# Loading the first rows of a rotation kernel in three pieces instead of two

## Chip, cores, metric

The kernel runs on one core of one Trainium2 chip. The metric is the device time of an execution in microseconds (us). A kernel is timed in rounds that alternate with the kernel before on the same chip. A profile covers one execution, and its span is some 1.8 us shorter than the time. Several figures below come from the trace's single packet records (start, duration and size of every packet) where no table of stretches shows them.

## The reference

The output is the input with both image axes reversed:

```python
x = randn(32, 3, 256, 256)                 # float32
out = rot90(x, k=2, axes=(-2, -1))         # out[.., i, j] = x[.., 255-i, 255-j]
```

The 96 images are 25.17 MB. They have to be read once and written once, so 50.33 MB pass through the DMA engines.

## The kernel before

The images are taken as three strips, A, Bt and Ct, of 32 images each. A strip is 128 rows of 16384 floats: every image is cut into four rows of 64 KB, one to each SBUF partition. VectorE reverses every row in place through a buffer T, and the store writes the four rows of an image in reverse order.

```python
G = 32
E = L // 4                                  # 16384 floats: 64 KB a row
x4 = x.rearrange("b c h w -> (b c) (h w)").rearrange(
    "(g n) (s e) -> g (n s) e", n=G, s=4)   # rows are 64 KB apart in memory
# ...
def load(t, g, lo, hi, queue=nc.sync):
    return queue.dma_start(out=t[:, lo:hi], in_=x4[g][:, lo:hi])
# ...
TAIL = 1536
HEAD = 512                                  # 2 KB of each row
load(A, 0, 0, HEAD, nc.scalar)
load(A, 0, HEAD, E)
load(Bt, 1, 0, E)
body = load(Ct, 2, 0, E - TAIL)
load(Ct, 2, E - TAIL, E)
inside(A)                                   # 12 copies on VectorE
LEAD = 128
store(A, 0, 0, LEAD)
first = store(A, 0, LEAD, E)                # made to wait for `body`
# ...
for g, t in ((1, Bt), (2, Ct)):
    inside(t)
    store(t, g, 0, E)
```

The large store of A is issued only when Ct's first load, `body`, has landed, so the loads come first and the stores after them. And VectorE's first copy of a strip reads the end of the row, which the largest load brings.

## Time and profile before

| | before |
|---|---|
| time, median of the first 3 runs | 122.09 us (121.94 to 122.15) |
| span of the profile | 120.2 us |
| sixteen DMA engines, share of the span with a packet | 97.6% |
| VectorE busy | 37% |
| VectorE's first copy starts | 22.6 us |

The DMA engines are the bound. Each has eight rows of each large load, and handles a row as one packet. The useful view is therefore the table of stretches, laid around the moments at which all sixteen engines take their next row (a "wave"). In such a stretch, DMA share times length is the mean packet time that one engine took on, and GB/s times length is the bytes, hence the number of packets. The prediction shows these lines.

### The profile page before, as it was taken

Reading aid. Unit: us, or ns where it says so; the run is one execution under the profiler, and the core shown is the slowest. Engines: PE = TensorE matmul, PEld = TensorE weight load, DVE = VectorE, ACT = ScalarE, POOL = GpSimd, SP = SyncE. Lnnn points to the kernel's source line nnn. Section 1 sums busy time; section 2 is a strip of 40 time slices with the busy share of each in tenths; the row PEclk is TensorE's granted clock in tenths of the full one; section 3 lists DMA queues with packets and bytes.
Section 4 is the critical chain, followed back from the end, with each engine's and each line's share of the span. In section 5 each row is a group of like instructions: output and inputs, shape, how many; then the busy total and the mean of one; then the engine's idle time right before and its main releaser. Section 6 shows DMA issues by size and latency. Waiting matters only on the chain.

```text
span 120.2 us, 97 instructions
## 1 busy us (share of the span) xinstructions
DVE 44.2 (37%) x36; POOL 0.2 (0%) x4
## 2 busy tenths in 40 slices
DVE  0000000499995099999059999500000000000000
POOL 0000000000000000000000000000000000000000
DMA  9888988899889879979499777988898889888990
GB/s 338 349 349 349 698 349 349 360 654 393 349 349 633 382 316 553 395 316 633 178 452 693 346 346 346 693 349 349 349 698 349 349 349 698 349 349 349 654 393 0
DMA packets 1296, 50.33 MB, mean 419 GB/s; under 512 B 144, under 2 KB 272, under 8 KB 528
## 3 DMA queue, kind: packets, MB, share of 16 engines
q1 hardware_dynamic: 1152, 50.07, 97.0%
q10 hardware_dynamic: 144, 0.26, 0.6%
HBM read 25.17 MB, written 25.17 MB: 419 GB/s over the span
## 4 chain that ended last, share of the span: by engine, by line
DMA 34%; DVE 25%; another core or an unknown queue 4%; issue 1%; SPq 0%; DVEq 0%
DMA Bt<-in_x_dram 34%; DVE T L52 8%; DVE Bt L52 8%; DVE Ct L52 8%; SPq L55 0%; DVEq L52 0%
## 5 line engine op out<-in xcount | busy, mean ns | idle before, releaser
L52 DVE COPY T<-A 128x2048 f32<-128x2048 f32 x4 | 4.9, 1226 | 22.7 <-DMA A<-in_x_dram 22.6
L52 DVE COPY T<-Ct 128x2048 f32<-128x2048 f32 x4 | 4.9, 1227 | 4.5 <-DMA Ct<-in_x_dram 4.4
L52 DVE COPY T<-Bt 128x2048 f32<-128x2048 f32 x4 | 4.9, 1226 | 4.4 <-DMA Bt<-in_x_dram 4.3
L52 DVE COPY Bt<-Bt 128x2048 f32<-128x2048 f32 x4 | 4.9, 1227 | 0.1
L52 DVE COPY A<-A 128x2048 f32<-128x2048 f32 x4 | 4.9, 1227 | 0.1
L52 DVE COPY A<-T 128x2048 f32<-128x2048 f32 x4 | 4.9, 1227 | 0.1
L52 DVE COPY Bt<-T 128x2048 f32<-128x2048 f32 x4 | 4.9, 1227 | 0.1
L52 DVE COPY Ct<-T 128x2048 f32<-128x2048 f32 x4 | 4.9, 1227 | 0.1
L52 DVE COPY Ct<-Ct 128x2048 f32<-128x2048 f32 x4 | 4.9, 1227 | 0.1
L100 POOL MEMSET const-bfloat16-1.0<- 128x1 bf16 x1 | 0.1, 101 | 0.0
L100 POOL MEMSET const-uint8-127<- 128x1 uint8 x1 | 0.1, 101 | 0.0
L100 POOL MEMSET const-float32-0.0<- 128x1 f32 x1 | 0.1, 98 | 0.2 <-issue 0.2
L100 POOL MEMSET const-float32-1.0<- 128x1 f32 x1 | 0.1, 98 | 0.0
## 6 DMA issues: line engine op xcount, KB each, us to landing
out_dram<-A SPq DMA_DIRECT2D x1, 8128.0 KB, 21.1
A<-in_x_dram SPq DMA_DIRECT2D x1, 7936.0 KB, 21.9
Ct<-in_x_dram SPq DMA_DIRECT2D x1, 7424.0 KB, 57.9
Ct<-in_x_dram SPq DMA_DIRECT2D x1, 768.0 KB, 59.3
A<-in_x_dram ACTq DMA_DIRECT2D x1, 256.0 KB, 22.0
out_dram<-A SPq DMA_DIRECT2D x1, 64.0 KB, 35.2
Bt<-in_x_dram SPq DMA_DIRECT2D x1, 40.8
out_dram<-Bt SPq DMA_DIRECT2D x1, 39.8
```

The source lines that it names most:

```text
L52: tc.keep_in_program_order(nc.vector.tensor_copy(out=dst, in_=src))
L100: nc = _bacc.Bacc("TRN2", target_bir_lowering=False, num_devices=1)
```

## The change

The intent is that the first packets are short on both queues, so that the engines get going at once, with the large rows behind them.

```diff
     load(A, 0, 0, HEAD, nc.scalar)
-    load(A, 0, HEAD, E)
+    load(A, 0, HEAD, 2 * HEAD)
+    load(A, 0, 2 * HEAD, E)
     load(Bt, 1, 0, E)
```

## The prediction

> **What bounds the kernel now.** I read the page first, for who is busy.
>
> ```profile
> span 120.2 us, 97 instructions
> DVE 44.2 (37%) x36; POOL 0.2 (0%) x4
> DMA packets 1296, 50.33 MB, mean 419 GB/s; under 512 B 144, under 2 KB 272, under 8 KB 528
> q1 hardware_dynamic: 1152, 50.07, 97.0%
> q10 hardware_dynamic: 144, 0.26, 0.6%
> ```
>
> VectorE works 37% of the span; the sixteen DMA engines are taken 97.0 + 0.6 = 97.6% of it. Every byte must come in and go out once, and the change alters none of that, so all that it can touch is the 2.4% (2.9 us over all, start and end included) in which the DMA engines hold no packet, and the way their time divides into packets. q10 is ACT's load: 144 packets are 128 rows and 16 small ones for completion, nine on each engine. q1 is SyncE's: eight transfers of 144.
>
> Next, who waits, to see whether VectorE's idle time is a reason or a result.
>
> ```profile
> DVE T L52 <- DMA A<-in_x_dram: 22.6, 1, 22.6
> DVE T L52 <- DMA Ct<-in_x_dram: 4.4, 1, 4.4
> DVE T L52 <- DMA Bt<-in_x_dram: 4.3, 1, 4.3
> ```
>
> VectorE waits once for each strip, always for a load, so it keeps up. Its last copy ends at about 76.7 us, while the stores of the first strip are still on the queue. The strips' arrival is only important in so far as the DMA engines never run dry.
>
> Then SyncE's own instructions in the timeline, for the start and for the turn from loads to stores.
>
> ```profile
> 0.73 0.39 SPq L55 DMA_DIRECT2D A<-in_x_dram  x1
> 1.18 0.42 SPq L55 DMA_DIRECT2D Bt<-in_x_dram  x1
> ...
> 26.39 33.78 SPq L58 DMA_DIRECT2D out_dram<-A  x2
> ```
>
> The first load is issued in 0.39 us, and about 0.45 us lies between two issues. (ACT issues its 2 KB piece at the same 0.73 us.) The second row says that the big store of A is out by 60.2 us. The question is whether the queue has work all the way, and the table of stretches answers it (columns: stretch, length, VectorE, GpSimd, clock, DMA share, GB/s). A stretch counts packets that begin in it, so I chose stretches around the waves in which all sixteen engines change packets.
>
> ```profile
> 1.20:1.75 0.55, 0.00 (x0) 0.00 (x0) 1.00 0.00 0
> 1.75:2.15 0.40, 0.00 (x0) 0.00 (x0) 1.00 7.23 2381
> 2.75:2.90 0.15, 0.00 (x0) 0.00 (x0) 1.00 0.98 423
> 4.70:5.35 0.65, 0.00 (x0) 0.00 (x0) 1.00 3.73 1613
> 24.10:24.75 0.65, 0.65 (x1) 0.00 (x0) 1.00 3.72 1613
> 59.25:60.25 1.00, 0.00 (x0) 0.00 (x0) 1.00 1.03 430
> 118.70:119.10 0.40, 0.00 (x0) 0.00 (x0) 1.00 0.02 0
> 119.10:120.18 1.08, 0.00 (x0) 0.00 (x0) 1.00 0.00 0
> ```
>
> - No packet begins before 1.75 us. In 1.75 to 2.15, 2381 GB/s for 0.40 us is 952 KB, which is 15 rows of 62 KB. Their time is 7.23 x 0.40 x 16 / 15 = 3.08 us each. The sixteenth engine begins in 2.75 to 2.90 and takes 0.98 x 0.15 x 16 = 2.35 us. The ACT pieces are not there: they wait until the big row is through.
> - At 4.70 to 5.35, 16 rows of 62 KB and 16 pieces of 2 KB start (1613 x 0.65 = 1048 KB = 16 x 64 KB): 3.73 x 0.65 = 2.42 us per engine for both. A 64 KB row of Bt (24.10 to 24.75) takes 3.72 x 0.65 = 2.418 us.
> - So the first wave costs about 3.08 - 2.34 = 0.74 us too much (2.34 being 62 KB at the steady pace), on fifteen engines. Afterwards the pace is steady.
> - At 59.25 to 60.25, the tail of Ct: 430 KB are 70 packets of 6 KB, 1.03 x 1.00 x 16 / 70 = 235 ns each. From 6 KB at 235 ns and 64 KB at 2418 ns, a packet costs 9 ns plus its bytes at 27.2 GB/s; sixteen engines make 435 GB/s.
> - The last completions begin by 119.10, and 1.08 us follows to the end of the span.
>
> The bound is therefore the stream of packets on each engine, from 1.76 us to 119.05: 3.146 MB per engine at 27.2 GB/s is 115.6 us, 72 data packets at 9 ns are 0.65, nine completion packets under 0.1, the start-up 0.74. That gives 117.1 of 117.3 us.
>
> **What the Trainium skill says.** "DMA: Bandwidth & Descriptors", section Bandwidth, puts the fabric's ceiling at 16 x 32 B x 850 MHz = 435.2 GB/s; the fit above gives 435, so nothing is to be had from the steady part. The same page, section Queues, rings and completion order, says that an engine takes its queues in turn, a whole packet at a time; the trace agrees, with one 2 KB piece after each 62 KB row at 4.70 to 5.35. Its section Issuing engines are not separate DMA queues says that issuing from several engines saves only the sequencer's time, since all run on the same sixteen engines. Its section Latency and other measured facts gives about 600 ns to the first byte for a transfer issued from SyncE or ACT; here the issue ends at 1.12 and the first packet begins at 1.76, 0.64 us later.
>
> **The change, part by part.**
> 1. Removed: the single load of 62 KB per row. Added: one of 2 KB and one of 60 KB in its place. Bytes are unchanged. Each engine has eight rows, so eight more packets at 9 ns, plus one completion packet of about 9 ns: 8 x 9 + 9 = 81 ns. These lie on the path, because each engine's stream sets the end: +0.08 us.
> 2. Added: one issue on SyncE, 0.45 us. All later loads are issued 0.45 us later (Bt at about 1.63 instead of 1.18). The queue holds work until then (step 4), so +0.00 on the path. The stores wait for data and for Ct's load, not for this.
> 3. Moved: the first 0.5 MB. Every engine begins with 2 KB pieces of both queues in turn. At (9 + 75) = 84 ns a piece, the sixteen pieces of an engine take 1.34 us, and only then do the 60 KB rows begin, near 3.1 us without the start-up and near 3.9 us with it. The order of the bytes changes, not their number: 0.00.
> 4. Does an engine run dry? Its first packets come 1.76 - 0.73 = 1.03 us after the issue. The 60 KB load, issued at 1.18, is there at about 2.2 us. The eight SyncE pieces alone last to 1.76 + 0.67 = 2.43 even without any start-up, with ACT's to 3.1. No gap: 0.00.
> 5. The start-up of 0.74 us is what the change could aim at. I take it for a delay of the first reads that is paid once, however long the first packet is: a first packet of 2 KB would last 0.08 + 0.7 us in place of 2.34 + 0.74. The engine that started late, near 2.8, paid nothing and still finished its row together with the others, which looks as if no data moved before about 2.5 us for anybody. I give a part of it a chance: expected gain 0.15 us.
> 6. VectorE: the last byte of A is still behind the same number of bytes, so it starts at 22.6 to 22.7 us. Its slack behind Bt (4.3 us) and Ct (4.4 us) absorbs that.
>
> Sum: +0.08 - 0.15 = -0.07, hence 122.09 - 0.07 = 122.0 us.
>
> **Rivals.**
> - The start-up belongs to large first packets (sixteen reads of 62 KB set off at once) and short ones avoid it. For it: 3.08 against 2.34 us, and that the sixteenth engine, alone in starting, took 2.35. Against: the early engines' lost time looks like one delay common to them all. The time would be 122.09 - 0.74 + 0.08 = 121.4 us.
> - Short first packets pay the delay more than once, or the 60 KB rows come later than I reckon, so an engine stands still for another start-up: 122.09 + 0.08 + 0.74 = 122.9 us. For it: the trace has no run of short HBM reads at the very start. Against: Ct's 6 KB rows are loaded back to back at the full rate.
> - The early pieces release something sooner. Against: VectorE's first copy needs the end of the row, which is in the 60 KB load. That is worth 0.
> - The split puts the engines out of step, or in step, at the turn to the stores, where the slowest of them sets when the stores go out. The engines' completions at the end fall within 0.4 us (all begin in 118.70 to 119.10), so the mean can move against the slowest by 0.2 us either way.
>
> **Range and chances.** Most likely 122.0 us. The favourable rival gives the low side, 121.4; the other side is +0.08, a spread effect of 0.2 and the three runs' own spread of 0.2: 122.5. The whole gap of 2% is 2.4 us, three times the start-up, and a loss of that size would need several starts paid in full. Chances: faster 0.01, within 2% 0.98, slower 0.01.
>
> **What would show it.** Packets of 2 KB alone in the first microseconds, the first big rows between 3 and 4 us (step 3); no stretch without work after 2 us (step 4); 1440 packets in all, and q10's share unchanged or a little above 0.6% (step 1); VectorE's first copy at 22.6 to 22.7 (step 6), the wait for Bt near 4.3; the span 120.1 to 120.3. A first copy of VectorE near 22.0 would be the first rival, one near 23.3 the second. I am wrong if the time moves by over 0.6 us, or if it moves and the first 23 us do not show it.

## The result

| | before | after |
|---|---|---|
| time, median of 6 runs | 122.08 us (121.94 to 122.15) | 122.62 us (122.36 to 123.05) |
| ratio | | 1.0049 (95% interval 1.0029 to 1.0068) |
| span of the profile | 120.2 us | 120.9 us |

A ratio is the mean time of one kernel's runs over that of the other's of the same rounds, so it is not quite the ratio of the medians quoted. The change loses about 0.5 us. That is within 2%, as forecast, but clear of noise, on the other side from the forecast, and outside its range of 121.4 to 122.5.

The page of the kernel after:

```profile
span 120.9 us, 99 instructions
DVE 44.2 (37%) x36; POOL 0.2 (0%) x4
DMA packets 1440, 50.33 MB, mean 416 GB/s; under 512 B 160, under 2 KB 288, under 8 KB 672
q1 hardware_dynamic: 1296, 50.07, 96.6%
q10 hardware_dynamic: 144, 0.26, 0.7%
```

The bytes and VectorE's work are those of before, with 144 packets more (128 pieces of 2 KB and 16 completions). What VectorE waited for, after:

```profile
DVE T L52 <- DMA A<-in_x_dram: 23.1, 1, 23.1
DVE T L52 <- DMA Ct<-in_x_dram: 4.4, 1, 4.4
DVE T L52 <- DMA Bt<-in_x_dram: 4.3, 1, 4.3
```

The first strip is 0.5 us later (23.1 instead of 22.6), while the two later waits are the same to 0.1 us. So the loss arises before 23 us and is then carried along. SyncE's own timeline shows the carrying. Its store of Bt is issued as soon as Ct's first load has let A's store go. First before, then after:

```profile
60.27 0.55 SPq L58 DMA_DIRECT2D out_dram<-Bt  x1
```

```profile
60.66 0.55 SPq L58 DMA_DIRECT2D out_dram<-Bt  x1
```

From that issue to the end of the span it is 59.9 us before and 60.2 after. In all 18 profiles it is 59.9 to 60.2, while the issue itself ranges from 60.1 to 62.6. The end is set by the moment at which Ct's first load has landed on *every* engine, that is, by the slowest of the sixteen.

What happened before 23 us is in the table of stretches (columns: stretch, length, VectorE, GpSimd, clock, DMA share, GB/s). First a wave of the kernel before, then the kernel after:

```profile
7.10:7.80 0.70, 0.00 (x0) 0.00 (x0) 1.00 3.47 1498
```

```profile
1.75:2.60 0.85, 0.00 (x0) 0.00 (x0) 1.00 0.81 147
2.60:3.42 0.82, 0.00 (x0) 0.00 (x0) 1.00 0.96 350
3.42:4.10 0.68, 0.00 (x0) 0.00 (x0) 1.00 3.94 1611
5.80:6.65 0.85, 0.00 (x0) 0.00 (x0) 1.00 2.76 1157
8.15:8.90 0.75, 0.00 (x0) 0.00 (x0) 1.00 3.18 1311
10.50:11.30 0.80, 0.00 (x0) 0.00 (x0) 1.00 3.00 1229
12.95:13.70 0.75, 0.00 (x0) 0.00 (x0) 1.00 3.05 1311
15.25:15.95 0.70, 0.00 (x0) 0.00 (x0) 1.00 3.24 1404
17.50:18.25 0.75, 0.00 (x0) 0.00 (x0) 1.00 3.02 1311
```

- Before, a 62 KB row and a 2 KB piece take 3.47 x 0.70 = 2.43 us in the third wave, the steady pace; the second wave, from 4.70 us in the prediction's lines, has it already (2.42).
- After, the short pieces begin at once. Up to 2.60 us there are 147 x 0.85 = 125 KB, or 61 of them, at 0.81 x 0.85 x 16 / 61 = 181 ns each. From 2.60 to 3.42 there are 140, at 0.96 x 0.82 x 16 / 140 = 90 ns. Undisturbed they take 84. The remaining 55 come with the first rows.
- A 60 KB row takes 3.02 x 0.75 = 2.27 us when undisturbed (last line). The five waves ahead of it take more: 2.37 (3.94 x 0.68 less the 55 short pieces and the completion packets), then 2.35, 2.39, 2.40 and 2.29. Their excess is 0.10 + 0.08 + 0.12 + 0.13 + 0.02 = 0.45 us per engine. I call these the slow waves. The kernel before has none after its first wave.

The start itself cost 0.42 us per engine after: the 256 short pieces took 0.81 x 0.85 + 0.96 x 0.82 + 55 x 0.084 / 16 = 1.77 us in place of 16 x 0.084 = 1.34. Before it was 15 x 0.74 / 16 = 0.69 us. So in these two profiles the mean engine gained 0.27 at the start, then lost 0.45 in the slow waves and 0.08 in the added packets: +0.26 us. This sum leaves part of the 0.5 us open. Engines that get their first packet later, and the slowest engine's distance from the mean, can account for it; neither was measured by itself. By the trace's packet records, the last large row of A ends at 21.90 us on average and at 22.15 on the slowest engine before, and at 22.37 and 22.72 after.

### The profile page after: what moved, and what is told of

The parts are those of the page before. It is cut to its first block, busy times and chain, and to the rows that moved or that the text cites. A ratio compares the mean times of both kernels' runs of the same rounds, so it can differ in the third digit from the quotient of the medians.

```text
span 120.9 us, 99 instructions
## 1 busy us (share of the span) xinstructions
DVE 44.2 (37%) x36; POOL 0.2 (0%) x4
## 2 busy tenths in 40 slices
DMA packets 1440, 50.33 MB, mean 416 GB/s; under 512 B 160, under 2 KB 288, under 8 KB 672
## 4 chain that ended last, share of the span: by engine, by line
DMA 34%; DVE 25%; another core or an unknown queue 4%; issue 1%; SPq 1%; DVEq 0%
DMA Bt<-in_x_dram 34%; DVE T L52 8%; DVE Bt L52 8%; DVE Ct L52 8%; SPq L55 1%; DVEq L52 0%
## 5 line engine op out<-in xcount | busy, mean ns | idle before, releaser
L52 DVE COPY T<-A 128x2048 f32<-128x2048 f32 x4 | 4.9, 1227 | 23.2 <-DMA A<-in_x_dram 23.1
```

The costliest lines, as they stand in the source:

```text
L52: tc.keep_in_program_order(nc.vector.tensor_copy(out=dst, in_=src))
```

## The experiments

Theory S was that short first packets leave the engines in a state that slows the rows behind them. Rival P was that one load more costs 0.5 us wherever it stands. Rival Q was that short packets on two queues at once are the trouble. All experiments change the kernel after, except where said.

### The short load behind the large one

```diff
     load(A, 0, 0, HEAD, nc.scalar)
-    load(A, 0, HEAD, 2 * HEAD)
     load(A, 0, 2 * HEAD, E)
+    load(A, 0, HEAD, 2 * HEAD)
```

> The same three loads as in the change, but SyncE issues the 60 KB load first and its 2 KB load behind it: as many loads, packets, issues and waits as in the changed kernel, and large first packets as in the kernel before. Theory S (short first packets leave the sixteen engines in a state in which their next waves of large rows are slowed, about 0.45 us per engine in the profile of the change, while a large first row gets that over in one wave): the first wave costs some 0.7 us too much, the later ones nothing, and the time is that of the kernel before plus the 0.08 us of the added packets, 122.1 to 122.3. Rival P (the added load costs 0.5 us by itself, wherever it stands): 122.5 to 122.7.

Measured: 122.09 us (before on that chip 121.97; ratio 1.0005, interval 0.9990 to 1.0020). The stretches of its first two waves:

```profile
1.70:2.25 0.55, 0.00 (x0) 0.00 (x0) 1.00 5.29 1787
4.60:5.30 0.70, 0.00 (x0) 0.00 (x0) 1.00 3.36 1448
```

The first wave, of 60 KB rows, takes 5.29 x 0.55 = 2.91 us, the second with a 2 KB piece 3.36 x 0.70 = 2.35, and nothing is slow after that. As many loads, packets and issues as in the change cost nothing measurable. Rival P is out: the order is what costs. VectorE's first copy came at 22.1 us here, 0.5 us earlier than in the kernel before, and its wait for Bt grew from 4.3 to 5.0 us; the time did not follow. So the first copy alone does not tell the time.

### All on one queue

```diff
-    load(A, 0, 0, HEAD, nc.scalar)
+    load(A, 0, 0, HEAD)
     load(A, 0, HEAD, 2 * HEAD)
     load(A, 0, 2 * HEAD, E)
```

> All three loads of the changed kernel on SyncE, in its order (2 KB, 2 KB, 60 KB). Theory S: short packets still come first, so slow waves follow and the time stays near 122.6, plus up to 0.45 us if the extra issue counts. Rival Q (two queues with short packets at the same time are what hurts): back to about 122.1 to 122.2, with no slow waves after the short packets.

Measured: 124.57 us, ratio 1.0211. Neither theory had this. The stretches:

```profile
1.70:3.40 1.70, 0.00 (x0) 0.00 (x0) 1.00 0.87 284
3.40:4.30 0.90, 0.00 (x0) 0.00 (x0) 1.00 1.95 728
4.30:5.60 1.30, 0.00 (x0) 0.00 (x0) 1.00 0.00 0
5.60:6.30 0.70, 0.00 (x0) 0.00 (x0) 1.00 2.90 1053
```

From 3.40 to 4.30, 655 KB begin: ten 60 KB rows and 20 short pieces. Then nothing begins until 5.60. By the packet records, six engines first got a large row between 5.6 and 6.3 us, and stood idle for about two microseconds. Rival Q is out: with one queue the rows behind the short pieces are slow as well (the twelve that begin from 5.60 to 6.30 take 2.90 x 0.70 x 16 / 12 = 2.71 us each, undisturbed 2.27). ACT's queue may help in the change because SyncE's large load is then its second and not its third; the next run tests this.

### The same with a middle piece of 16 KB

```diff
-    load(A, 0, HEAD, 2 * HEAD)
-    load(A, 0, 2 * HEAD, E)
+    load(A, 0, HEAD, 9 * HEAD)
+    load(A, 0, 9 * HEAD, E)
```

on the one-queue kernel.

> All three loads on SyncE, with a middle one of 16 KB of each row. With a middle one of 2 KB (124.6) six engines stood idle from about 3.5 to 6 us, between their short packets and the large rows. If the cause is that the descriptors of SyncE's third load come late, and the short packets are over before them: sixteen KB a row last eight times as long (about 4.9 us per engine), nothing stands idle, and the time is 122.1 to 122.4. If three loads in a row on one queue cost 2 us whatever their size: 124 or more.

Measured: 122.11 us (before 122.06; ratio 1.0004). No engine stood idle. With enough work ahead of it the third load on one queue is free, so the idle time of the one-queue kernel was short pieces running out before the large rows were there. Why these were so late, three microseconds and more after their issue, no run shows.

### A single load

```diff
-    load(A, 0, 0, HEAD, nc.scalar)
-    load(A, 0, HEAD, 2 * HEAD)
-    load(A, 0, 2 * HEAD, E)
+    load(A, 0, 0, E)
```

> A in a single 64 KB load on SyncE, ACT issues nothing. Shows what a short piece is worth at all. Theory S: large first packets, a start-up of about 0.7 us in the first wave and nothing after it, nine packets per engine fewer than before at 9 ns: 122.0 to 122.2. If ACT's 2 KB piece does something useful in the kernel before, this one is slower than 122.3.

Measured: 122.18 us, ratio 1.0016 (interval 0.9998 to 1.0034). The expected time came out. The short piece of the kernel before is worth some 0.2 us by this ratio; the interval allows nothing, and 0.4.

### Other sizes of the middle piece

```diff
-    load(A, 0, HEAD, 2 * HEAD)
-    load(A, 0, 2 * HEAD, E)
+    load(A, 0, HEAD, K * HEAD)      # K = 3, 5, 9: 4, 8, 16 KB
+    load(A, 0, K * HEAD, E)
```

> SyncE's middle load has 16 KB of each row in place of 2 KB, the last one 46 KB. Theory S: the first packet is longer, and the disturbance is over after some of the 16 KB packets, so less is left for the large rows: between before and after, 122.2 to 122.5. Rival P: 122.6, as the count of packets is the same.

> SyncE's middle load has 8 KB of each row, between the 2 KB of the change (122.6) and 16 KB (122.2). If the loss fades as the first packets get longer: 122.2 to 122.4. If it comes with the third load itself: 122.6.

> SyncE's middle load has 4 KB of each row (16 KB brought back 122.2, 2 KB cost 122.6). If the loss grows as the first packets get shorter: 122.3 to 122.6, with slow waves of the large rows of less weight than in the change. If it is a matter of the short pieces' being there at all: 122.6.

Measured: 122.17 us with 16 KB, 122.13 with 8 KB and 122.13 with 4 KB (ratios 1.0008, 1.0010, 1.0004, all with 1 in the interval). I had expected the loss to fade gradually, with 122.3 to 122.6 at 4 KB. It is gone at 4 KB already, as far as these intervals of about 0.2 us either way can tell. By the packet records the waves of large rows behind 4 KB still have a little excess (0.08 us in all), and none worth naming behind 8 or 16 KB. The size decides, then: of the sizes tried, only 2 KB loses clearly.

### One short load only

```diff
-    load(A, 0, 0, HEAD, nc.scalar)
-    load(A, 0, HEAD, 2 * HEAD)
-    load(A, 0, 2 * HEAD, E)
+    load(A, 0, 0, HEAD)
+    load(A, 0, HEAD, E)
```

> ACT issues nothing; SyncE loads 2 KB of each row, then 62 KB: one short packet a row instead of two, as many loads as the kernel before. Theory: short first packets bring slow waves or a lagging engine, 122.3 to 122.8. If the descriptors of the second load come late as those of the third did on one queue, engines stand idle and it is 123 to 125. Rival: only two short loads together do it, 122.0 to 122.2.

Measured: 122.32 us (before 122.09; ratio 1.0019, interval 0.9998 to 1.0040). This is not clear of noise. By the packet records no engine stood idle; the first wave of 62 KB rows took 2.66 us instead of 2.34, the next ones the steady time. The short pieces lost 0.35 us per engine against 84 ns each, and the first rows 0.32; the sum, 0.67, is close to the 0.69 of the kernel before. It looks as if the rows paid what the short pieces had left over of the start-up.

### The distance between the rows

All sixteen engines go through rows that start a multiple of 64 KB apart. These kernels read A's rows at another distance. Their outputs are wrong, which doesn't matter for the times. Bytes, packets and issues stay.

```diff
+    PITCH = E + 1024                 # 68 KB; +2048: 72 KB; +512: 66 KB
+    wide = x.rearrange("b c h w -> (b c h w)")[0:P * PITCH].rearrange(
+        "(p e) -> p e", e=PITCH)
     def load(t, g, lo, hi, queue=nc.sync):
+        if g == 0:
+            return queue.dma_start(out=t[:, lo:hi], in_=wide[:, lo:hi])
```

> Wrong result on purpose: the changed kernel, but the rows of A are read at a distance of 68 KB instead of 64 KB, so that the sixteen engines, which all go through their rows in step, no longer read addresses a multiple of 64 KB apart. Same bytes, packets and issues. Theory H (the slow waves and the first wave's loss are the engines hitting the same parts of HBM at once, because their rows are 64 KB apart): the packets of A come at the steady pace from the first, VectorE's first copy starts 0.4 to 0.9 us earlier than in the change (23.1), and the time falls to 121.7 to 122.2. Rival L (a loss of the start that does not depend on addresses): unchanged, 122.6.

> Wrong result on purpose: the kernel before with A's rows read at a distance of 68 KB. Theory H: the first wave takes about 2.4 us instead of 3.04, VectorE starts near 22.0 instead of 22.6, and the time falls to 121.4 to 121.8. Rival L: unchanged, 122.1.

The kernel after at 68 KB: 122.16 us, ratio 1.0012 (interval 0.9997 to 1.0026), VectorE's first copy at 22.5. Its waves:

```profile
5.80:6.35 0.55, 0.00 (x0) 0.00 (x0) 1.00 4.12 1787
8.10:8.60 0.50, 0.00 (x0) 0.00 (x0) 1.00 4.53 1966
10.35:10.90 0.55, 0.00 (x0) 0.00 (x0) 1.00 4.12 1787
```

Each is 2.27 us (4.12 x 0.55; 4.53 x 0.50): the slow waves are gone. But the kernel before at 68 KB took 122.23 us (ratio 1.0016, interval 1.0000 to 1.0033), not the 121.4 to 121.8 expected. Its first wave:

```profile
1.70:2.40 0.70, 0.00 (x0) 0.00 (x0) 1.00 4.49 1451
```

These are 16 rows of 62 KB at 4.49 x 0.70 = 3.14 us, as slow as ever. The distance thus bears on the slow waves and not on the start-up, and half of theory H fell. At 68 KB the kernel before (1.0016) and the change (1.0012) take the same time within their intervals.

The change again, the change on other rows at the same 64 KB (`load(A, 1, ...)`, wrong) and 72 KB ran on one chip:

> The changed kernel itself once more, on the chip of the next two runs, to compare with. If the loss is the change's own and not one chip's or one moment's: 122.4 to 122.9 beside 122.0 for the kernel before, with slow waves of A's large rows up to some 10 us or beyond.

> Wrong result on purpose: the changed kernel, A's three loads read the second strip's rows instead of the first's; the distance of the rows stays 64 KB. A control for the 68 KB run: other addresses, the same distance. Theory H (rows 64 KB apart, after short first packets, make the slow waves): they are there again, 122.4 to 122.9. Rival C (any other addresses would have ended them by chance): no slow waves, 122.0 to 122.2.

> Wrong result on purpose: the changed kernel with A's rows read at a distance of 72 KB. Theory H: as with 68 KB, no slow waves of the 60 KB rows (mean below 2.28 us in each wave), short packets at the start still cost 0.4 to 0.6 us per engine, time 122.0 to 122.3. If the 68 KB run was luck: slow waves again, 122.4 or more.

Measured: 122.70, 122.59 and 122.52 us. The loss is the change's own (ratio 1.0048 for the change again). Other rows at 64 KB lose as much (1.0041), so it is not that any other addresses would do. The fourth wave, first with the other rows at 64 KB (16 rows of 60 KB, 2.40 x 1.00 = 2.40 us), then at 72 KB (1.90 x 1.20 = 2.28):

```profile
10.55:11.55 1.00, 0.00 (x0) 0.00 (x0) 1.00 2.40 983
```

```profile
10.30:11.50 1.20, 0.00 (x0) 0.00 (x0) 1.00 1.90 819
```

At 72 KB the slow waves were gone as expected, but the time, ratio 1.0033, was a miss. What VectorE waited for in this profile:

```profile
DVE T L52 <- DMA A<-in_x_dram: 23.2, 1, 23.2
```

Its waves are at the steady pace, and yet the strip is 0.6 us later than before. By the packet records its slowest engine ends A 0.70 us behind the mean of the sixteen (before: 0.26). Such a lag is there at the start: its first 60 KB row begins at 4.67 us, the others' from 3.5 to 4.6.

So two repeats and a third distance went with the question of what was chance:

> Wrong result on purpose: the 68 KB kernel once more. Theory H: no slow waves of the 60 KB rows (each wave's mean below 2.28 us). If the short packets' start is equally good each time, 122.1 to 122.2 again; if the slowest engine's lag is chance, anything from 122.1 to 122.6, with VectorE's first copy later where the time is longer.

> Wrong result on purpose: the 72 KB kernel once more. Theory H: no slow waves. If its 122.5 belongs to the lag of one engine at the start and comes each time: 122.4 to 122.6 with VectorE's first copy near 23.2; if it was chance: 122.1 to 122.3.

> Wrong result on purpose: the changed kernel with A's rows 66 KB apart. Theory H: no slow waves of the 60 KB rows; time 122.1 to 122.5 according to the slowest engine's lag. If 66 KB shows them, the distance must be off by more than 2 KB to end them, or theory H is wrong.

Measured: 122.28, 122.30 and 122.36 us (ratios 1.0012, 1.0016, 1.0019). The waves stayed near the steady pace; in the two repeats one wave each was a little over the limit I had set (2.295 and 2.286 us against 2.28). This time the 72 KB kernel's runs went from 122.14 to 122.56 (the first time from 122.35 to 122.63), and the profiled one, with the first copy at 23.2 again, was the slowest of them. So the lag may differ from one execution to the next. But both profiles at 72 KB have it (0.70 and 0.58 us) and the three at 66 and 68 KB have less (0.25 to 0.46), so whether it is chance or belongs to this distance stays open.

All eight profiles with two short pieces on two queues, with the excess of their first six waves of 60 KB rows over 2.267 us, from the packet records:

| rows of A | slow waves, us per engine | ratio to before |
|---|---|---|
| 64 KB, the change | 0.45 | 1.0049 |
| 64 KB, the change again | 0.25 | 1.0048 |
| 64 KB, other rows | 0.27 | 1.0041 |
| 66 KB | 0.00 | 1.0019 |
| 68 KB | 0.01 | 1.0012 |
| 68 KB again | 0.03 | 1.0012 |
| 72 KB | 0.02 | 1.0033 |
| 72 KB again | 0.03 | 1.0016 |

The mean ratio is 1.0046 at 64 KB and 1.0018 at the other distances. Against 122.06 us these are +0.56 and +0.22 us, so by estimate some 0.34 us of the loss goes with the 64 KB distance; a single ratio is known to about 0.25 us either way. The packet records agree: on the mean engine, A's last large row ends at 22.36 to 22.40 us in the three profiles at 64 KB and at 21.88 to 22.26 (mean 22.02) in the other five, 0.36 us earlier.

Of the other 0.22 us, 0.08 is the estimate for the added packets. For the remaining 0.14 there are two candidates that no run separates: the lag of the slowest engine (0.25 to 0.74 us in the eight profiles, 0.26 before), and the other distance itself, at which the kernel before lost as much.

No version beat the kernel before. The best were level with it: the short load behind the large one (1.0005), 4 KB in the middle (1.0004), and one queue with 16 KB (1.0004).

## Why the prediction was wrong

**The bound was right.** Bytes, VectorE's work and its later waits did not move, and what went wrong in the first 23 us went through to the end. The prediction's two signs of being wrong did not show: the time moved by 0.5 us, not over 0.6, and the first 23 us do show it. The sign named for the second rival, a first copy near 23.3 us, was nearly met, at 23.1, though no engine stood still for another start-up.

**Step 1, added packets, +0.08 us: right as far as tested.** 1440 packets came, and the same number in the other order cost no more than a ratio of 1.0005 can hold.

**Step 2, the issue, 0.00: right.** The same run shows it.

**Step 3, "The order of the bytes changes, not their number: 0.00": this is the step that failed.** With 2 KB pieces of both queues first, the following waves of large rows were slow: 0.45 us in the profile of the change, 0.25 and 0.27 in the two others at 64 KB. I took the steady pace of the trace before for a property of the rows. In the kernel before it is the pace after a first wave of 62 KB rows. The runs show that it also depends on the distance of the rows and on how short the packets before them are. Why this is so is not shown.

**Step 4, no gap, 0.00: right for the change, by luck of the queue.** No stretch without work opened. With the same pieces on SyncE alone it did, for two microseconds on six engines. My reckoning that a load is there 1.03 us after its issue did not hold for the third load.

**Step 5, a start-up paid once, gain 0.15 us: the size was near by luck, the reading was wrong, and the gain did not reach the time.** Data moved at once, with 61 pieces begun by 2.60 us, slowed to 181 ns each. The mean start-up fell from 0.69 to 0.42 us in the profile of the change; by the packet records it was 0.42 to 0.70 in the eight profiles with two short pieces. But the engines no longer paid alike (in the profile of the change single 2 KB pieces took up to 731 ns), and the end waits for the slowest. That is the fourth rival's mechanism, sized there at 0.2 us either way; in the profile of the change again the slowest engine was 0.74 us behind the mean, three times the lag before.

**Step 6, first copy at 22.6 to 22.7: wrong**, 23.1, as a consequence of steps 3 and 5.

The first rival expected short packets to avoid the start-up. They avoid a part of it at most, and at 64 KB the rows behind them lose more than that. The second expected engines to stand idle, which only the one-queue kernel did. The range had no room for both a loss in the waves and a lag, and it left out the second rival's own 122.9.

## What to carry to other kernels

When sixteen engines run at a constant pace, ask what brought them into that state before changing what they do first: the pace may belong to the order, not to the packet. A transfer that all engines share ends with the slowest one, so look at the spread as well as the mean. Short pieces ahead of a large load must last until the large load has arrived on every engine, or engines stand idle, as six did in the one-queue kernel.

## What the Trainium skill lacked or had wrong

- "DMA: Bandwidth & Descriptors", section Issuing engines are not separate DMA queues, says that issuing from several engines saves only the sequencer's time. Here moving one 2 KB load from ACT to SyncE took the time from 122.6 to 124.6 us, with six engines idle for about two microseconds, where an issue takes 0.45 us.
- The same page, section Latency and other measured facts, has copies between HBM tensors that are slow at row pitches of 2 MiB and more, and nearly at full rate at 512 KiB. It says nothing of 64 KB. Here rows 64 KB apart load at full pace (2.27 us for 60 KB) when settled, but after 2 KB first packets they took up to 2.40 us on average in some waves, and at 66, 68 and 72 KB at most 2.30.
- No page that I found has the slow first microsecond: in the profile of the change short packets began at once, but took 181 ns each up to 2.60 us and 90 ns after that, and a large first row took 0.6 to 0.8 us longer than later ones, at 64 and at 68 KB.
